# A last projection by seven products of half blocks, with sums of its weights prepared beside earlier stages

## The chip, the cores and the metric

The kernel runs on one core of one Trainium2 chip. The metric is the device time of one execution in microseconds; a kernel's time is the median of its runs. Only the last projection, the place where its weights are made ready, and the way one gated unit is written differ between the two kernels; inputs, outputs and all other stages are the same.

## What is computed

A layer of a streaming encoder: 2048 tokens of 1024 channels in float32, one layer, one batch. In the reference, cut to what matters:

```python
h = rms_norm(x, norm_g) * (1.0 + scale) + shift
u = h @ w_in
glu_in, gate_a, q, k, v, gate_b, m_a, m_b = split(u)
y_a = conv_branch(glu_in, gate_a)              # GLU, causal convolution of width 31, LayerNorm, projection
o   = stick_breaking_attention(norm(q), norm(k), v)
y_b = (o * silu(gate_b)) @ w_sb_out
y   = sigmoid(m_a) * y_a + sigmoid(m_b) * y_b
x   = x + gate * (y @ w_out)                   # w_out: 1024 x 1024
```

The last line is the last projection. Its product has the shape 1024 x 1024 by 1024 x 2048 in the kernel's orientation (channels on partitions, tokens along the free axis).

## The kernel before

Every large product is made of float32r halves: an operand is split into `hi`, its rounded value, and `lo`, what is left, and a product takes three matmuls (hi by hi, hi by lo, lo by hi; `mm3`). ScalarE casts `hi`, and GpSimd (for weights) or VectorE (for the rest) subtracts `lo`. Tokens go in four chunks of 512 (`CH`, `NCH`), channels in eight blocks of 128 (`KC`).

Weights come in **pieces** of 128 x 1024 (`piece`, `load_piece`, `split_into`): each half of 512 columns is loaded by SyncE into a `wl` tile (two of these, shared by all pieces), cast into `whi` (L102) and subtracted into `wlo` (L103). There are three slots for split pieces: two in the pool `wpa`, one in `wpb`, taken in turn, so a piece takes the slot that the third piece before it had. A piece is issued as soon as a slot and the `wl` tiles are free, as far as the scheduler's order on each engine lets it. SyncE, ScalarE, GpSimd and VectorE work their instructions off in order: one that waits holds all behind it.

The stages, in the order of TensorE's work:

- the first stage: normalised input, and the projections `glu`, `silu_block` (gate A, part of gate B), queries, keys and values; VectorE works off the convolution's taps beside it. `glu(j)` makes one channel block of the gated unit: `B_GLU_B` goes through a sigmoid on ScalarE (L660), `B_GLU_A` is multiplied with it on VectorE (L667). Both write `u`, whose even and odd tokens lie apart, as the convolution wants them
- the stage beside the LayerNorm, from about 620 to 780 us: `v_group(5)`, `gate_b(2)`, `gate_b(3)`, and three merge gates (`merge_gate`, of `blocks[:NEARLY]`). A generator `ln_all` puts a step of the LayerNorm after each of their tiles; it loads the convolution's output (`cv`), squares it (`sq`, L800), sums and casts (`hl`, L770), normalises, gates, and stores `za` (L834). Each gate tile is read by ScalarE into `vsg` (L857, L868) and stored (L859, L869)
- attention, with the other merge gates as a filler on TensorE in an order written out by hand; at its end the first chunk's `y_tiles`
- the tail. For each chunk: `y_tiles` (192 matmuls `p` by the weights `wc`, L1066 to L1072 for the evictions and the splitting of y into `yh` and `yl`), then eight output tiles, `out_tile` (24 matmuls `po` each, 192 for the chunk), evicted by one VectorE operation that multiplies by `gate` and adds x (L1083). The projection's weights `wo` are loaded and split once, in the first chunk (L1191), and stay: `wo0` in the pool `wr`, the others in `wor`, which is declared for the right side of the memory

In the tail TensorE alternates: y of chunk 0, output of chunk 0, y of chunk 1, and so on.

## Time and profile before

| | us |
|---|---|
| median of three runs | 1858.18 |
| lowest and highest run | 1856.52, 1859.29 |
| the profiled execution | 1858.59 |
| its span in the trace | 1856.5 |

The page gives each engine's busy time as a share of the span, then its chain of waits: from the last instruction back to what released it, step by step. A row of a group has the line, the engine, the operation, the tile written and those read, the count, the busy time and the mean of one, and the idle time of that engine ahead of it with what ended it. PE is TensorE's matmuls, PEld its weight loads, DVE VectorE, ACT ScalarE, POOL GpSimd, SP SyncE; a name such as SPq is that engine's queue. Rows of a timeline have start, duration, engine, line, operation, tiles, count and the idle time ahead. A matmul of 512 columns shows 0.39 us in such a row, but matmuls overlap: the step from one start to the next is what counts.

### The profile page before, as it was taken

How to read it: one execution, taken by the hardware profiler on the slowest of the kernel's cores; microseconds unless marked ns; L12 is line 12 of the kernel's file. 1: busy time of each engine (PE TensorE's matmuls, PEld its weight loads, DVE VectorE, ACT ScalarE, POOL GpSimd, SP SyncE). 2: the span in 40 equal slices, each digit the busy share in tenths (PEclk: the TensorE clock that was granted, in tenths of full speed). 3: DMA queues.
4: the chain of work that ended last, by engine and by line, in shares of the span. 5: the costliest groups of instructions: out<-in, count | busy, mean ns of one | idle time of the engine just before them, and what ended most of it. 6: DMA issues, size and time to landing. Idle time of an engine off the chain costs nothing.

```text
span 1856.5 us, 27230 instructions
## 1 busy us (share of the span) xinstructions
PE 1788.4 (96%) x9612; PEld 1510.5 (81%) x9612; DVE 1229.2 (66%) x1696; ACT 825.9 (44%) x1896; POOL 668.6 (36%) x883
## 2 busy tenths in 40 slices
PE   6899999999999999999999999999999899999999
PEld 5888889899898888788787777778788677888887
DVE  7645578888879555377777777767777895334241
ACT  5465113232131234377777776767777752010110
POOL 0253112112111133276656666666666731010100
PEclk9999999999999999999999999999999999999999
DMA  8563402315042454423231323231322446353532
GB/s 286 175 188 103 142 29 68 104 50 167 23 119 92 146 189 150 160 80 104 62 95 65 100 67 99 78 94 55 100 71 83 140 155 210 102 164 93 167 93 80
DMA packets 117596, 211.08 MB, mean 114 GB/s; under 512 B 15442, under 2 KB 27730, under 8 KB 117460
## 3 DMA queue, kind: packets, MB, share of 16 engines
q1 hardware_dynamic: 116308, 207.24, 35.9%
q10 hardware_dynamic: 1152, 2.10, 0.3%
q8 instruction: 76, 1.25, 0.3%
q14 instruction: 60, 0.49, 0.1%
HBM read 137.98 MB, written 71.30 MB: 113 GB/s over the span
## 4 chain that ended last, share of the span: by engine, by line
PE 77%; DVE 7%; POOL 5%; ACT 4%; issue 4%; DMA 3%; SPq 0%; DVEq 0%; ACTq 0%; POOLq 0%
PE pd L115 43%; PE po L115 9%; PE p L115 8%; PE av L115 5%; PE pT L120 5%; PE z L115 5%; POOL w L962 3%; DVE sc L955 3%; DMA wl<-in_w_qkv_dram 1%; DVE tlo L989 1%; ACT z L951 1%; POOL wlo L103 1%; PE pt L120 1%; ACT w L950 1%; DMA qst<-qhi 1%
## 5 line engine op out<-in xcount | busy, mean ns | idle before, releaser
L962 POOL TENSOR_TENSOR w<-w,sc 128x512 f32<-128x512 f32 (+1 forms) x320 | 361.4, 1130 | 252.6 <-DVE sc L955 179.5
L115 PE MATMUL pd<-hhi,whi 128*128 128x512 f32 x1024 | 410.6, 401 | 1.0 <-ACT vsg L868 1.0
L115 PE MATMUL pd<-hhi,wlo 128*128 128x512 f32 x1024 | 400.9, 391 | 0.0
L115 PE MATMUL pd<-hlo,whi 128*128 128x512 f32 x1024 | 400.6, 391 | 0.0
L955 DVE TENSOR_TENSOR_SCAN sc<-z,sc,w 128x512 f32<-128x512 f32 x192 | 244.9, 1279 | 91.3 <-ACT z L951 83.3
L103 POOL TENSOR_TENSOR wlo<-wl,whi 128x512 fp32r<-128x512 f32 x88 | 131.4, 1502 | 406.8 <-ACT whi L102 405.6
L950 ACT ACTIVATE w<-z 128x512 f32<-128x512 f32 (+1 forms) x320 | 172.3, 538 | 126.6 <-PE z L115 102.8
L115 PEld LDWEIGHTS pd<-hhi,wlo 128*128 128x128 f32 x1024 | 192.2, 188 | 41.6 <-POOL wlo L103 0.2
L115 PEld LDWEIGHTS pd<-hhi,whi 128*128 128x128 f32 x1024 | 194.0, 189 | 34.9 <-ACT vsg L868 1.4
L115 PEld LDWEIGHTS pd<-hlo,whi 128*128 128x128 f32 x1024 | 192.9, 188 | 33.9
L989 DVE TENSOR_TENSOR tlo<-pT,thi 128x512 fp32r<-128x512 f32 (+1 forms) x320 | 184.0, 598 | 35.4 <-ACT thi L988 32.9
L115 PE MATMUL z<-kt,q 128*128 128x512 f32 (+2 forms) x640 | 193.0, 383 | 5.5 <-DVE sc L955 4.0
L988 ACT CAST thi<-pT 128x512 fp32r<-128x512 f32 (+1 forms) x320 | 165.2, 527 | 61.2 <-PE pT L120 57.5
L120 PE MATMUL pT<-ident,w 128*128 128x128 f32 x1088 | 173.1, 275 | 9.7 <-POOL w L962 9.4
L120 PEld LDWEIGHTS pT<-ident,w 128*128 128x128 f32 x1088 | 137.4, 141 | 45.6 <-POOL w L962 14.5
L115 PE MATMUL pd<-whi,hhi 128*128 128x256 f32 x608 | 169.7, 287 | 3.7 <-ACT hhi L131 2.0
L951 ACT ACTIVATE z<-z 128x512 f32<-128x512 f32 (+1 forms) x320 | 171.8, 537 | 0.0
L115 PE MATMUL pd<-whi,hlo 128*128 128x256 f32 x608 | 167.0, 285 | 2.5 <-DVE hlo L131 1.9
L115 PE MATMUL pd<-wlo,hhi 128*128 128x256 f32 x608 | 154.0, 284 | 0.0
L959 DVE TENSOR_TENSOR_SCAN sc<-z,tri 128x512 f32<-128x512 f32 (+3 forms) x128 | 104.3, 819 | 60.9 <-ACT z L951 40.4
L115 PE MATMUL av<-tlo,vt 128*128 128x512 f32 (+1 forms) x320 | 122.8, 384 | 13.4 <-DVE tlo L989 10.2
L115 PEld LDWEIGHTS z<-kt,q 128*128 128x128 f32 x640 | 109.5, 189 | 25.4 <-DVE sc L955 6.4
(284 smaller groups left out, 3104.8 us busy)
## 6 DMA issues: line engine op xcount, KB each, us to landing
wl<-in_w_in_dram SPq DMA_DIRECT2D x64, 256.0 KB, 2.9
wa<-in_w_ada_dram SPq DMA_DIRECT2D x24, 512.0 KB, 5.2
wl<-in_w_qkv_dram SPq DMA_DIRECT2D x36, 256.0 KB, 2.8
xt<-in_x_n_dram SPq DMA_DIRECT2D x16, 512.0 KB, 5.5
vst<-st SPq DMA_DIRECT2D x64, 128.0 KB, 2.0
kt<-kst SPq DMA_DIRECT2D x32, 256.0 KB, 2.8
vt<-vst SPq DMA_DIRECT2D x32, 256.0 KB, 2.7
q<-qst SPq DMA_DIRECT2D x32, 256.0 KB, 2.8
```

What stands on the lines that cost most here:

```text
L103: (lo_eng or nc.gpsimd).tensor_tensor(out=lo[:, s], in0=wl, in1=f(hi[:, s]), op=ALU.subtract)
L115: i = nc.tensor.matmul(*a, **k)
L120: i = nc.tensor.transpose(*a)
L950: nc.scalar.activation(out=w[:, lo:], in_=z[:, lo:], func=AF.Sigmoid, scale=HD ** -0.5)
L951: nc.scalar.activation(out=z[:, lo:], in_=z[:, lo:], func=AF.Sigmoid, scale=-HD ** -0.5)
L955: nc.vector.tensor_tensor_scan(out=s[:, 1:], data0=z, data1=w, initial=s[:, 0:1], op0=ALU.mult, op1=ALU.bypass)
L959: nc.vector.tensor_tensor_scan(out=s[:, lo + 1:], data0=z[:, lo:], data1=tri[:, :CH - lo], initial=1.0, op0=ALU.mult, op1=ALU.max)
L962: nc.gpsimd.tensor_tensor(out=w[:, lo:], in0=w[:, lo:], in1=s[:, lo:CH], op=ALU.mult)
L988: nc.scalar.copy(out=thi[:, :n], in_=pT[:, :n])
L989: nc.vector.tensor_tensor(out=tlo[:, :n], in0=pT[:, :n], in1=f(thi[:, :n]), op=ALU.subtract)
```

## The change

**The last projection** works on pairs of chunks. The 1024 x 1024 weight matrix is cut into 2 x 2 blocks of 512, y of a pair of chunks into 2 x 2 blocks of 512 channels by 512 tokens. The table `SEVEN` gives for each of seven products the blocks of the weights that it sums (A), those of y (B), and the outputs to which it is added or from which it is subtracted. Blocks are named (row or input half, column half, sign); a product of one block each has a single term. A product is four row blocks of four input blocks, three matmuls each: 48. Each result is added by VectorE into one or two of the outputs (12 additions of four row blocks for a pair), with `gate` or its negative `ngate`; an output tile `acc` starts as x and is stored after its last product (`LASTS`). y stays in float32 and isn't split by itself.

**Operands.** A of five products is a sum of two blocks. These are made ahead: `prepare` loads two half tiles of `w_out` for each, adds them on GpSimd, splits the sum, and stores the pair to memory (`ws`, 512 KB); ten calls make two each. Four calls stand in the first stage (two in `glu(0)`, one in the first `silu_block`, one in `glu(1)`), six in the stage beside the LayerNorm (one behind each call of `v_group`, `gate_b` and `merge_gate`). Each takes one of the three slots for pieces, and `wl` tiles. A of the two other products (4 and 3) is loaded from `w_out` when it is used and split then. B is summed on GpSimd where it has two terms, cast on ScalarE and subtracted on VectorE. The operands of the next product are issued ahead of the current one; two sets of tiles (`za`, `zb` and `oa`, `ob`) take turns.

**The gated unit.** `glu` now reads PSUM by parity and writes `u` contiguously, where before it read PSUM in sequence and wrote `u` with a step.

```diff
+    SEVEN = {
+        2: (((1, 0, 1), (1, 1, 1)), ((0, 0, 1),), ((1, 0, 1), (1, 1, -1))),
+        1: (((0, 0, 1), (1, 1, 1)), ((0, 0, 1), (1, 1, 1)), ((0, 0, 1), (1, 1, 1))),
+        6: (((1, 0, 1), (0, 0, -1)), ((0, 0, 1), (0, 1, 1)), ((1, 1, 1),)),
+        4: (((1, 1, 1),), ((1, 0, 1), (0, 0, -1)), ((0, 0, 1), (1, 0, 1))),
+        7: (((0, 1, 1), (1, 1, -1)), ((1, 0, 1), (1, 1, 1)), ((0, 0, 1),)),
+        3: (((0, 0, 1),), ((0, 1, 1), (1, 1, -1)), ((0, 1, 1), (1, 1, 1))),
+        5: (((0, 0, 1), (0, 1, 1)), ((1, 1, 1),), ((0, 0, -1), (0, 1, 1))),
+    }
+    LASTS = {(1, 0): 4, (1, 1): 3, (0, 0): 5, (0, 1): 5}
+    H = KC // 2
...
+        sums = [(m, j) for m in SEVEN if len(SEVEN[m][0]) == 2 for j in range(H)]
+
+        def prepare():
+
+            npiece[0] += 1
+            pool = wpb if npiece[0] % 3 == 0 else wpa
+            for t in [pool.tile([P, 2, CH], F32R, tag=t, name=t) for t in ("whi", "wlo")]:
+                m, j = sums.pop(0)
+                w = [wpa.tile([P, CH], F32, tag="wl", name="wl", bufs=2) for _ in range(2)]
+                for i, (r, c_, _) in enumerate(SEVEN[m][0]):
+                    nc.sync.dma_start(w[i], w_out[j + H * r][:, c_ * CH:(c_ + 1) * CH])
+                nc.gpsimd.tensor_tensor(
+                    out=w[0], in0=w[0], in1=w[1],
+                    op=ALU.add if SEVEN[m][0][1][2] > 0 else ALU.subtract)
+                nc.scalar.copy(out=t[:, 0, :], in_=w[0])
+                nc.gpsimd.tensor_tensor(out=t[:, 1, :], in0=w[0], in1=f(t[:, 0, :]),
+                                        op=ALU.subtract)
+                ws_d[m, j] = dram(f"ws{m}_{j}", [P, 2, CH], F32)
+                nc.sync.dma_start(ws_d[m, j], f(t))
...
                 def at_(g):
-                    return u[:, :, g * CH // 2:(g + 1) * CH // 2].rearrange("p t m -> p m t")
+                    return u[:, :, g * CH // 2:(g + 1) * CH // 2]
+
+                def by_parity(ps):
+                    return ps.rearrange("p (m t) -> p t m", t=2)
 
                 w = piece(w_in[B_GLU_B + j])
+                if j < 2:
+                    prepare()
...
-                    nc.scalar.activation(out=at_(g), in_=ps.rearrange("p (m t) -> p m t", t=2),
-                                         func=AF.Sigmoid)
+                    nc.scalar.activation(out=at_(g), in_=by_parity(ps), func=AF.Sigmoid)
...
                 w = piece(w_in[B_GLU_A + j])
+                if j < 1:
+                    prepare()
...
-                    nc.vector.tensor_tensor(out=at_(g), in0=ps.rearrange("p (m t) -> p m t", t=2),
-                                            in1=at_(g), op=ALU.mult)
+                    nc.vector.tensor_tensor(out=at_(g), in0=by_parity(ps), in1=at_(g),
+                                            op=ALU.mult)
...
             def silu_block(blk, dst, after=None):
                 w = piece(w_in[blk])
+                if blk == B_GA:
+                    prepare()
...
             def v_group(grp):
                 w2 = [piece(w_qkv[grp, i]) for i in range(2)]
+                prepare()
...
             def gate_b(j):
                 w = piece(w_in[B_GB + j])
+                prepare()
...
             def merge_gate(blk, dst):
                 w = piece(w_in[blk])
+                prepare()
...
-            return yp.tile([P, CH], F32, tag="io", name=name, bufs=4)
+            return yp.tile([P, CH], F32, tag="io", name=name, bufs=8)
...
-                nc.vector.tensor_tensor(out=ma, in0=ma, in1=mb, op=ALU.add)
-                hi = yp.tile([P, CH], F32R, tag=f"yh{j}", name=f"yh{j}")
-                lo = yp.tile([P, CH], F32R, tag=f"yl{j}", name=f"yl{j}")
-                nc.scalar.copy(out=hi, in_=ma)
-                nc.vector.tensor_tensor(out=lo, in0=ma, in1=f(hi), op=ALU.subtract)
-                y[0].append(hi)
-                y[1].append(lo)
+                y[ch, j] = (yr if ch % 2 else yp).tile([P, CH], F32, tag=f"y{j}", name=f"y{j}")
+                nc.vector.tensor_tensor(out=y[ch, j], in0=ma, in1=mb, op=ALU.add)
                 yield
 
-        def out_tile(ch, j, y, psum):
...
+        def operands(m, ch):
+
+            q = "zo"[turn[0] % 2]
+            turn[0] += 1
+            A, B = [], []
+            for j in range(H):
+                A.append(operand(q, "a", j))
+                if (m, j) in ws_d:
+                    nc.sync.dma_start(f(A[j]), ws_d[m, j])
+                else:
+                    (r, c_, _), = SEVEN[m][0]
+                    w = io("w")
+                    nc.sync.dma_start(w, w_out[j + H * r][:, c_ * CH:(c_ + 1) * CH])
+                    split_z(w, A[j], (nc.gpsimd, nc.vector)[j % 2])
+            for kc in range(H):
+                B.append(operand(q, "b", kc))
+                t = combined(SEVEN[m][1], lambda t: y[ch + t[1], kc + H * t[0]],
+                             lambda: yp.tile([P, CH], F32, tag="io", name="sum", bufs=8),
+                             nc.gpsimd)
+                nc.scalar.copy(out=B[kc][:, 0, :], in_=t)
+                nc.vector.tensor_tensor(out=B[kc][:, 1, :], in0=t, in1=f(B[kc][:, 0, :]),
+                                        op=ALU.subtract)
+            return A, B
...
+        def product(m, ch, A, B, psum):
+            for j in range(H):
+                ps = psum("po")
+                for kc in range(H):
+                    s = slice(kc * P, (kc + 1) * P)
+                    mm3(ps, A[j][:, 0, s], A[j][:, 1, s], B[kc][:, 0, :], B[kc][:, 1, :],
+                        kc == 0, kc == H - 1)
+                for r, c_, sign in SEVEN[m][2]:
+                    row, g = j + H * r, ch + c_
+                    ts_ = slice(g * CH, (g + 1) * CH)
+                    if (row, g) not in acc:
+                        acc[row, g] = ya.tile([P, CH], F32, tag="acc", name="acc", bufs=12)
+                        nc.sync.dma_start(acc[row, g], x_t[row][:, ts_])
+                    o = acc[row, g]
+                    nc.vector.scalar_tensor_tensor(
+                        out=o, in0=ps, scalar=(gate if sign > 0 else ngate)[:, row:row + 1],
+                        in1=o, op0=ALU.mult, op1=ALU.add)
+                    if LASTS[r, c_] == m:
+                        nc.sync.dma_start(out_t[row][:, ts_], o)
...
-            for j in range(KC):
-                if ch == 0:
-                    wo[j] = resident(wr if j == 0 else wor, w_out[j], f"wo{j}")
-                out_tile(ch, j, y, psum)
+        for ch in (0, 2):
             if ch:
-                y = ([], [])
-                ygen = y_tiles(ch, za, zb, psum, y)
...
+                za3, zb3 = load_za(3), load_zb(3)
+                steps(y_tiles(2, za, zb, psum, y))
+                steps(y_tiles(3, za3, zb3, psum, y))
+            order = list(SEVEN)
+            nxt = operands(order[0], ch)
+            for i, m in enumerate(order):
+                A, B = nxt
+                if i + 1 < len(order):
+                    nxt = operands(order[i + 1], ch)
+                elif ch == 0:
+                    za, zb = load_za(2), load_zb(2)
+                product(m, ch, A, B, psum)
```

What stands where. First ScalarE's rows beside the LayerNorm, from the last tile of `v_group` through gate B 2 up to the start of gate B 3. Before (`st` is the value tile's cast, `vsg` a gate tile; `whi_6949` is gate B 3's piece, `whi_7174` the first merge gate's):

```order
L102 CAST whi_6949<-wl_6951 128x512
L102 CAST whi_6949<-wl_6955 128x512
L329 CAST st_6717<-pd_6668 128x8x64
L102 CAST whi_7174<-wl_7176 128x512
L857 ACTIVATE vsg_6789<-pd_6764 128x512
L102 CAST whi_7174<-wl_7180 128x512
```

and then, after eight rows of the LayerNorm:

```order
L857 ACTIVATE vsg_6851<-pd_6826 128x512
L800 ACTIVATE sq0_6867<-cv0_6523 128x512
L800 ACTIVATE sq1_6870<-cv1_6525 128x512
L800 ACTIVATE sq2_6873<-cv2_6527 128x512
L857 ACTIVATE vsg_6916<-pd_6891 128x512
L800 ACTIVATE sq3_6876<-cv3_6529 128x512
L770 CAST hl_6888<-t1_6883 128x512
L102 CAST whi_7359<-wl_7361 128x512
L857 ACTIVATE vsg_6945<-pd_6920 128x512
L102 CAST whi_7359<-wl_7365 128x512
```

In the change, the same stretch from the second tile of gate B 2 (L906 is the gate tile's sigmoid, L847 the square, L817 the cast `hl`, L233 the cast of a prepared sum; `whi_7069` is gate B 3's piece):

```order
L906 ACTIVATE vsg_6971<-pd_6946 128x512
L233 CAST wlo_6865<-wl_6875 128x512
L847 ACTIVATE sq0_6987<-cv0_6623 128x512
L847 ACTIVATE sq1_6990<-cv1_6625 128x512
L847 ACTIVATE sq2_6993<-cv2_6627 128x512
L906 ACTIVATE vsg_7036<-pd_7011 128x512
L847 ACTIVATE sq3_6996<-cv3_6629 128x512
L906 ACTIVATE vsg_7065<-pd_7040 128x512
L817 CAST hl_7008<-t1_7003 128x512
L102 CAST whi_7069<-wl_7071 128x512
L102 CAST whi_7069<-wl_7075 128x512
L233 CAST whi_7079<-wl_7081 128x512
```

Gate B 3's casts stood ahead of gate B 2's first tile; now they stand behind all of its four tiles and behind `hl`.

SyncE there in the change (`ws` is the store of a prepared sum, `wl_7071` and `wl_7075` are the loads of gate B 3's piece, `gb2_1` gate B 2's third tile, L787 the LayerNorm's next input):

```order
L881 DMA za2_3_274<-lsg_6933 128x512
L237 DMA ws6_3_6882<-wlo_6865 128x1024
L881 DMA za3_3_278<-lsg_6940 128x512
L908 DMA gb2_2_193<-vsg_6971 128x512
L787 DMA cv2_6982<-cv2_165 128x2x256
L787 DMA cv3_6984<-cv3_166 128x2x256
L908 DMA gb2_1_192<-vsg_7036 128x512
L101 DMA wl_7071<-in_w_in_dram 128x512
L101 DMA wl_7075<-in_w_in_dram 128x512
L829 DMA gt_7128<-ga0_2_169 128x512
L829 DMA gt_7128<-ga1_2_173 128x512
L829 DMA gt_7131<-ga2_2_177 128x512
```

Before, gate B 3's loads stand ahead of all stores of gate B 2; now they stand behind the third one.

The same place one stage on, the loads of the third merge gate in the change (`wl_7713`, `wl_7717`; `mb0_2` is the second tile of the gate before it):

```order
L829 DMA gt_7681<-ga1_0_171 128x512
L881 DMA za2_1_272<-lsg_7506 128x512
L881 DMA za3_1_276<-lsg_7513 128x512
L237 DMA ws5_1_7547<-wlo_7530 128x1024
L919 DMA mb0_3_234<-vsg_7574 128x512
L829 DMA gt_7684<-ga2_0_175 128x512
L919 DMA mb0_2_233<-vsg_7622 128x512
L829 DMA gt_7684<-ga3_0_179 128x512
L101 DMA wl_7713<-in_w_in_dram 128x512
L101 DMA wl_7717<-in_w_in_dram 128x512
```

They too stand behind stores of the gate that runs then, and of the LayerNorm's `za`.

TensorE where the tail begins, before (y of the first chunk, then the first output tile):

```order
L115 MATMUL p2_16451<-zb2_15675,wc7h_16350 128x512 x2
L115 MATMUL p2_16451<-zb2_15675,wc7l_16351 128x512
L115 MATMUL p2_16451<-zb3_15683,wc7h_16350 128x512 x2
L115 MATMUL p2_16451<-zb3_15683,wc7l_16351 128x512
L115 MATMUL po_16535<-yh0_15937,wo0h_16523 128x512
L115 MATMUL po_16535<-yl0_15938,wo0h_16523 128x512
```

and in the change, where the first product begins:

```order
L115 MATMUL p2_16956<-ob2_16573,wc7h_16589 128x512 x2
L115 MATMUL p2_16956<-ob2_16573,wc7l_16590 128x512
L115 MATMUL p2_16956<-ob3_16581,wc7h_16589 128x512 x2
L115 MATMUL p2_16956<-ob3_16581,wc7l_16590 128x512
L115 MATMUL po_17024<-zb0_16984,za0_16976 128x512 x3
L115 MATMUL po_17024<-zb1_16987,za0_16976 128x512 x3
L115 MATMUL po_17024<-zb2_16990,za0_16976 128x512 x3
L115 MATMUL po_17024<-zb3_16993,za0_16976 128x512 x3
```

Those last rows of `p` are now y of the second chunk: both chunks of a pair are done before their seven products, and a product's matmuls take as weights a half of `za` (a sum of `w_out`) and as moving tile a half of `zb` (a block of y).

More of the change, by code (lines that the diff above doesn't have):

```diff
@@ L162, in trunk_kernel @@
     za_d = [[dram(f"za{j}_{g}", [P, CH], F32) for g in range(NCH)] for j in range(JC)]
+    ws_d = {}
     o_d = [[dram(f"o{j}_{g}", [P, CH], F32) for g in range(NCH)] for j in range(JC)]
@@ L1004, in av_mm @@
                 nc.sync.dma_start(o_d[h // 2][rc][a], oc[a])
-        wcs, wo = {}, {}
+        wcs = {}
         def resident(pool, src, name):
@@ L1015, in io, with split_z, operand @@
         def io(name):
-            return yp.tile([P, CH], F32, tag="io", name=name, bufs=4)
-        def split_z(o, t):
+            return yp.tile([P, CH], F32, tag="io", name=name, bufs=8)
+        def split_z(o, t, eng=nc.vector):
             nc.scalar.copy(out=t[:, 0, :], in_=o)
-            nc.vector.tensor_tensor(out=t[:, 1, :], in0=o, in1=f(t[:, 0, :]), op=ALU.subtract)
+            eng.tensor_tensor(out=t[:, 1, :], in0=o, in1=f(t[:, 0, :]), op=ALU.subtract)
+        def operand(q, half, i):
+            pool = yr if (q, half) == ("o", "b") else yp
+            return pool.tile([P, 2, CH], F32R, tag=f"{q}{half}{i}", name=f"{q}{half}{i}")
         def load_za(ch):
@@ L1024, in load_za @@
             for kc in range(JC):
-                t = yp.tile([P, 2, CH], F32R, tag=f"za{kc}", name=f"za{kc}")
+                t = operand("zooz"[ch], "a", kc)
                 o = io("n")
@@ L1034, in load_zb @@
             for kc in range(JC):
-                t = yp.tile([P, 2, CH], F32R, tag=f"zb{kc}", name=f"zb{kc}")
+                t = operand("zooz"[ch], "b", kc)
                 o = io("o")
@@ L1075, in y_tiles @@
-                yield
-        def out_tile(ch, j, y, psum):
-            ts_ = slice(ch * CH, (ch + 1) * CH)
-            xt = io("xt")
-            nc.sync.dma_start(xt, x_t[j][:, ts_])
-            ps = psum("po")
-            dense(ps, wo[j], y, KC)
-            nc.vector.scalar_tensor_tensor(out=xt, in0=ps, scalar=gate[:, j:j + 1], in1=xt,
-                                           op0=ALU.mult, op1=ALU.add)
-            nc.sync.dma_start(out_t[j][:, ts_], xt)
+                y[ch, j] = (yr if ch % 2 else yp).tile([P, CH], F32, tag=f"y{j}", name=f"y{j}")
@@ new lines, in y_tiles, with combined @@
+                nc.vector.tensor_tensor(out=y[ch, j], in0=ma, in1=mb, op=ALU.add)
+                yield
+        def combined(terms, part, tmp, eng):
+            if len(terms) == 1:
+                return part(terms[0])
+            t = tmp()
+            (a, b) = terms
+            eng.tensor_tensor(out=t, in0=part(a), in1=part(b),
+                              op=ALU.add if b[2] > 0 else ALU.subtract)
+            return t
+        turn = [0]
+        def operands(m, ch):
[20 more added lines that the diff above has]
+            return A, B
@@ new lines, in trunk_kernel @@
+        acc = {}
+        def product(m, ch, A, B, psum):
[17 more added lines that the diff above has]
+                        nc.sync.dma_start(out_t[row][:, ts_], o)
@@ L1101, in trunk_kernel @@
         nf = ny = 0
-        prev = held = ygen = wr = yp = None
-        y = ([], [])
+        prev = held = ygen = wr = yp = ngate = None
+        y = {}
         psum = lambda n: pd.tile([P, CH], F32, tag="pd", name=n)
@@ L1125, in others @@
             def others(q, half):
-                nonlocal nf, ny, ygen, wr, yp
+                nonlocal nf, ny, ygen, wr, yp, ngate
                 while nf < (int(due[2 * q + half + 1] + 0.001) if q < LAST else NF):
@@ L1140, in others @@
                         wcs[1] = load_piece(wpa, w_cs[1])
+                    ngate = yp.tile([P, KC], F32, name="ngate")
+                    nc.vector.tensor_scalar(out=ngate, in0=gate, scalar1=-1.0, scalar2=None,
+                                            op0=ALU.mult)
                     ygen = y_tiles(0, za, zb, lambda n: psum(n), y)
@@ L1176, in trunk_kernel, with steps @@
     with s3:
-        wor = s3.enter_context(tc.tile_pool(name="wor", reuse_waits="tile", bufs=1, side="right"))
+        yr = s3.enter_context(tc.tile_pool(name="yr", reuse_waits="tile", bufs=1, side="right"))
         pd = s3.enter_context(tc.tile_pool(name="pd3", reuse_waits="tile", bufs=2, space=PSUM))
         psum = lambda n: pd.tile([P, CH], F32, tag=n, name=n, bufs=4 if n == "po" else 2)
-        for ch in range(NCH):
-            if ch:
-                y = ([], [])
-                ygen = y_tiles(ch, za, zb, psum, y)
-            for _ in ygen:
-                pass
-            if ch + 1 < NCH:
-                za = load_za(ch + 1)
-                zb = load_zb(ch + 1)
-            for j in range(KC):
-                if ch == 0:
-                    wo[j] = resident(wr if j == 0 else wor, w_out[j], f"wo{j}")
-                out_tile(ch, j, y, psum)
+        def steps(gen):
+            for _ in gen:
+                pass
+        za, zb = load_za(1), load_zb(1)
+        steps(ygen)
+        steps(y_tiles(1, za, zb, psum, y))
+        ya = s3.enter_context(tc.tile_pool(name="ya", reuse_waits="tile", bufs=1, side="right"))
+        for ch in (0, 2):
+            if ch:
+                za3, zb3 = load_za(3), load_zb(3)
[10 more added lines that the diff above has]
+                product(m, ch, A, B, psum)
 def _layout(i):
```

## The prediction

> **What bounds the kernel now.** I read the busy shares and the chain that ended last first, then busy time by stretch of the stages that the change touches, then the chain over the last 320 us, and last single rows of the engines where PE's weights are made ready.
>
> ```profile
> PE 1788.4 (96%) x9612; PEld 1510.5 (81%) x9612; DVE 1229.2 (66%) x1696; ACT 825.9 (44%) x1896; POOL 668.6 (36%) x883
> ...
> PE pd L115 43%; PE po L115 9%; PE p L115 8%; PE av L115 5%; PE pT L120 5%; PE z L115 5%; POOL w L962 3%; DVE sc L955 3%; DMA wl<-in_w_qkv_dram 1%; DVE tlo L989 1%; ACT z L951 1%; POOL wlo L103 1%; PE pt L120 1%; ACT w L950 1%; DMA qst<-qhi 1%
> ```
>
> PE is busy for 96% of the span; nothing else comes near. A matmul taken away is worth its step wherever PE doesn't wait, and a wait added in front of PE costs in full. By stretch (us, busy of PE, PEld, DVE, ACT, POOL, clock, DMA share, GB/s):
>
> ```profile
> 200.00:250.00 50.00, 50.00 (x222) 41.39 (x221) 35.48 (x36) 6.79 (x10) 7.06 (x4) 1.00 0.21 72
> 657.60:674.00 16.40, 16.40 (x78) 13.54 (x78) 12.78 (x26) 8.43 (x13) 9.48 (x7) 1.00 0.63 199
> 674.00:690.00 16.00, 16.00 (x76) 13.38 (x75) 10.26 (x23) 5.18 (x10) 5.14 (x5) 1.00 0.77 240
> 690.00:720.00 30.00, 30.00 (x137) 24.92 (x136) 15.64 (x26) 11.52 (x19) 11.19 (x8) 1.00 0.47 152
> 720.00:752.00 32.00, 32.00 (x154) 26.85 (x153) 14.95 (x31) 13.09 (x22) 7.32 (x6) 1.00 0.38 137
> ```
>
> In the GLU stage (first row) and beside the LayerNorm (the others) PE never rests: the new preparation finds idle ACT and POOL there, but no idle PE that could swallow a late weight. In the tail, the row where the first output projection starts, then the chain (start, us, what):
>
> ```profile
> 1541.33 0.39 PE L115 MATMUL po<-yh,wo0h 128*128 128x512 f32 x1
> ```
> ```profile
> 1548.18 39.93 PE po L115 x170
> 1588.12 43.54 PE p L115 x192
> 1631.66 44.64 PE po L115 x192
> ...
> 1764.47 43.52 PE p L115 x192
> 1807.99 44.66 PE po L115 x192
> 1852.65 0.03 issue
> 1852.68 0.75 DVE xt L1083
> ```
>
> From 1588 us on it is matmuls alone: `p` (y, 192 of them) and `po` (last projection, 192) in turn, then one eviction and the store.
>
> **The change part by part.** *The tail.* The four projections take 46.8 (1541.33 to 1588.12; some of it waits for loads of `w_out`), 44.64, 44.64 and 44.66 us: 180.7. Seven products of 4 x 4 x 3 matmuls for each pair of chunks make 336; two pairs make 672 where 768 stood. Their step isn't in the trace, but both ends are:
>
> ```profile
> L115 PE MATMUL po<-yh,wo7l 128*128 128x512 f32 x32 | 12.7, 396 | 0.0
> ...
> L115 PE MATMUL po<-yh,wo0l 128*128 128x512 f32 x32 | 12.5, 390 | 0.0
> ```
>
> `p` goes at 43.52/192 = 0.2267 us; `po` at 44.64/192 = 0.2325, and of its weights `wo0`, the only one in a left-side pool, is as fast as `p`, the seven of the right-side pool 6 ns slower. The products' weights (`za`, `oa`) all lie in the left-side pool, so I take 0.2267; the moving half `ob` lies on the right, so 0.2333 stays as the other end. That makes 2 x 336 x 0.2267 = 152.3 us (156.8 at the other end): **28.4 us less** (23.9). After the last matmul two evictions stand where one stood (a product feeds up to two outputs): +0.75. Tail: **-27.7** (-23.2).
>
> That holds if operands are ready. One product lasts 48 x 0.2267 = 10.9 us. Prices:
>
> ```profile
> L1083 DVE SCALAR_TENSOR_TENSOR xt<-po,gate,xt 128x512 f32<-128x512 f32 x32 | 23.8, 750 | 102.2 <-PE po L115 89.5 <-DMA xt<-in_x_t_dram 7.9 <-DMA mb<-mb 4.8
> L1072 DVE TENSOR_TENSOR yl<-ma,yh 128x512 fp32r<-128x512 f32 x25 | 17.3, 692 | 18.2 <-ACT yh L1071 18.2
> ...
> L1040 POOL TENSOR_TENSOR o<-o,gb 128x512 f32<-128x512 f32 x12 | 16.8, 1406 | 200.3 <-DMA gb<-gb 90.3 <-DMA o<-o 75.9 <-ACT wo6h L102 34.0
> L1071 ACT CAST yh<-ma 128x512 fp32r<-128x512 f32 x25 | 15.5, 620 | 196.4 <-DVE ma L1068 196.4
> ...
> L1020 DVE TENSOR_TENSOR zb<-o,zb 128x512 fp32r<-128x512 f32 x12 | 9.7, 807 | 20.5 <-ACT zb L1019 20.2
> ```
>
> For a pair of chunks: DVE 48 evictions x 0.75 + 32 subtractions x 0.69 = 58.1 us of 76.2; POOL 20 sums and 4 subtractions x 1.41 = 34; ACT 36 casts x 0.62 = 22. Two operand sets alternate, so row j of A is reloaded when product i-1 is done with it and wanted a row less than two products later (19 us); a 512 KB load takes 5.2 us in the row below. B is wanted whole: a set is free when product i-1 ends, the sums can be made before, four casts and subtractions take 4 x 0.69 + 0.62 = 3.4 of 10.9 us.
>
> ```profile
> wa<-in_w_ada_dram SPq DMA_DIRECT2D x24, 512.0 KB, 5.2
> ```
> ```profile
> 25.00:40.00 15.00, 12.95 (x100) 12.43 (x100) 13.04 (x24) 9.97 (x20) 0.00 (x0) 1.00 0.96 336
> ```
>
> Loads and stores of the first pair (8.4 MB of prepared sums, 2.1 of plain halves, x, output, next z) are about 19 MB in 76 us, 250 GB/s, where 336 went through at 0.96 share. So I cost operands at 0; the 32 casts and 32 subtractions of `yh` and `yl` that go save nothing, since PE covered them.
>
> *GLU by parity.* Its two operations now read PSUM at a step of 2 and write in sequence:
>
> ```profile
> L660 ACT ACTIVATE u<-pd x16: 1085/1108/1118, 172.5 to 474.2; 128x512 f32<-128x512 f32 x16
> ```
> ```profile
> L667 DVE TENSOR_TENSOR u<-pd,u x16: 1083/1098/1116, 197.9 to 495.7; 128x512 f32<-128x512 f32 x16
> ```
>
> At best each falls to a plain 0.60/0.68 (0.42 us less), at worst stays or doubles; PE at 50.00 of 50 hides either. 0; without that cover 32 x 0.42 = 13 us either way.
>
> *The preparation.* Ten calls make 20 half pieces of sums: 40 loads, 20 stores of 512 KB, 40 POOL operations, 20 casts. Their own time hides (POOL 4 x 1.29 = 5.2 us per call in stretches with 10 to 20 idle). What doesn't hide is room: each call takes one of three slots for split weights and both `wl` tiles, so the next piece, which was split two pieces ahead, now waits for a slot until one ahead, on SP and ACT behind work that has waits of its own. Four calls stand in the GLU stage, where SP and ACT are nearly idle: I reckon the next piece ready 2 to 5 us before PE asks, 0, bounded by 3 us each. Six stand beside the LayerNorm. Gate B 3, row by row, before:
>
> ```profile
> 657.58 0.48 PE L115 MATMUL pd<-hhi,whi 128*128 128x512 f32 x1
> ```
> ```profile
> 655.58 1.14 ACT L102 CAST whi<-wl 128x512 fp32r<-128x512 f32 x2 [3.74 <-PE pd L115]
> ...
> 679.66 0.63 ACT L800 ACTIVATE sq<-cv 128x512 f32<-128x512 f32 x1 [3.94 <-DMA za<-lsg]
> 680.20 0.58 ACT L857 ACTIVATE vsg<-pd 128x512 f32<-128x512 f32 x1
> ...
> 684.45 0.62 ACT L770 CAST hl<-t 128x512 fp32r<-128x512 f32 x1 [3.16 <-DVE t L749]
> ```
> ```profile
> 681.53 0.33 SPq L859 DMA_DIRECT2D gb<-vsg  x1
> ```
> ```profile
> wl<-in_w_in_dram SPq DMA_DIRECT2D x6, 256.0 KB, 3.2
> ```
>
> Gate B 2 starts at 657.58 and has 96 matmuls at 0.2267 and about 1.1 us of LayerNorm ones, so gate B 3 starts near 680.5; its casts were done at 655.58 (gate B 2's take that place in the change: cast by 656.2, subtracted on POOL by 657.5, in time for its third matmul). In the change gate B 3's two loads stand on SP behind the store at 681.53, which waits for `vsg` at 680.20, and that for the LayerNorm's `sq`, held 3.94 us by a store. Loads issue at 681.9 and 682.2 and land 3.2 later, the first at 685.1; the casts stand behind `hl` (to 685.1), so 685.7, and the first POOL half is done 1.29 later, 687.0. PE's third matmul needs it, at 681.0: 6 us late, and the DMA share of 0.77 there with a 512 KB store and four new loads more makes that **8** (6 to 9). Of the three merge gates behind it, by the same count, the first is in time and the second has no slack, **1** (0 to 2). The third, before:
>
> ```profile
> 742.74 1.29 ACT L800 ACTIVATE sq<-cv 128x512 f32<-128x512 f32 x2 [2.22 <-DMA za<-lsg]
> ```
> ```profile
> 744.54 7.85 SPq L869 DMA_DIRECT2D mb<-vsg  x3
> ```
> ```profile
> 751.77 0.48 PE L115 MATMUL pd<-hhi,whi 128*128 128x512 f32 x1
> ```
>
> It starts at 751.77 and in the change its loads stand behind the first of those stores, whose `vsg` waits for that `sq`, and that for a `za` store; a sum and a subtraction of 1.29 each come before that store on POOL. So the loads issue 2.6 later than 744.9, land 3.2 later at 750.7, 1.91 for cast and subtraction makes 752.6, against a third matmul at 752.3; with DMA as busy as above I take **3.5** (0 to 7). All: **+12.5**, 6 to 18.
>
> **Sum.** 1858.59 (the profiled execution: span 1856.5 and 2.1 around it) - 27.7 + 12.5 = 1843.4; the median of the runs shown, 1858.18, is 0.4 below the profiled one: **1843 us**.
>
> **The rivals.** *All hidden* (1831): the loads are issued earlier than I read the queue, or DMA is quick enough. For it: 27.7 with nothing given back; against it: the 3.94 and 3.16 us waits above, which the new order puts ahead of the casts. *Every preparation holds its piece* (1852): six pieces lose 3.5 each, 1830.5 + 21, and the slower step and the GLU stage make up to 1857. For it: every piece has the same two `wl` tiles ahead of it; against it: a piece lasts 96 x 0.2267 = 21.8 us, and only where `vsg` waits for the LayerNorm do the loads come in its last quarter. *The products become DVE's* (slower): DVE's subtractions read two SBUF tiles while POOL makes the sums, as here:
>
> ```profile
> L830 DVE TENSOR_TENSOR lsg<-gt,cv x16: 697/1790/1811, 669.3 to 768.1; 128x512 f32<-128x512 f32 x16
> ```
>
> At 1.79 instead of 0.70 beside POOL, the 32 subtractions take 57.3, DVE 93.3 us of a pair against PE's 76.2: +17 twice, 1843 + 34 = 1877. It decides from a mean of 1.26 us (36 + 32 x 1.26 = 76.2) and makes the kernel slower from 1.55. Against it: beside L1040's POOL work the same subtraction took 0.807, and POOL is busy for 34 of 76 us. [...]
>
> **How the numbers follow.** Forecast 0.60, all hidden 0.15, every piece held 0.17 (0.07 of it beyond 1854.5), products DVE's 0.08 (0.02 of it only as far as no change). About 0.2%, 3.7 us, is what a measurement of this kernel can tell from no change: faster 0.85, same 0.09, slower 0.06. The range goes from everything hidden, 1831, to the tail at the slower step with 18 us of late weights: 1830.5 + 4.4 + 18 = 1853, and 1 of the GLU stage's bound, 1854.
>
> **What would show it.** Right: `po` comes to 672 matmuls at 0.227, PE without gaps from the second y on, and between 680 and 760 us one gap of 6 to 9 us before gate B 3, with a cast `whi` as its releaser, and a smaller one before the third merge gate; the attention stage unchanged but later. Wrong: gaps of PE before a product's first row, on a subtraction of `ob` or `zb` (then DVE or POOL is late) or on a load of `ws`; gaps in the GLU stage; a `po` step of 0.233; or no gap near 680.

## The result, and the profile after

| | us |
|---|---|
| before, median of 5 | 1858.18 (1856.52 to 1860.17) |
| after, median of 5 | 1876.31 (1870.66 to 1882.84) |
| ratio, 95% interval | 1.0092 (1.0063 to 1.0122) |
| profiled execution after, its span | 1882.84, 1881.1 |

The change makes the kernel slower, where 1843 us was forecast. The profiled execution is the slowest of the five, so the account below adds up to 24.6 us (1881.1 - 1856.5) and not to the 18 of the medians. The page after, engines and chain:

```profile
PE 1780.3 (95%) x9516; PEld 1503.2 (80%) x9516; DVE 1302.7 (69%) x1777; ACT 844.7 (45%) x1940; POOL 799.8 (43%) x971
...
PE 63%; DMA 9%; POOL 8%; DVE 8%; issue 5%; ACT 5%; SPq 1%; DVEq 0%; POOLq 0%; ACTq 0%
PE pd L115 32%; PE p L115 8%; PE po L115 7%; PE av L115 5%; PE pT L120 5%; PE z L115 5%; DMA wl<-in_w_out_dram 3%; POOL w L1012 3%; DVE sc L1005 2%; DMA wl<-in_w_in_dram 2%; POOL wlo L103 2%; POOL wl L230 1%; DMA wl<-in_w_qkv_dram 1%; ACT z L1001 1%; DMA gb<-gb 1%
```

PE has 96 matmuls fewer and is busy 8 us less, yet the span grew: the chain is PE for 63% of it where it was 77%, and loads of `w_out` and POOL's sums (L230) stand on it now. Busy time by stretch, in the columns of before:

```profile
600.00:650.00 50.00, 47.44 (x290) 43.03 (x289) 25.90 (x29) 10.10 (x17) 12.89 (x10) 0.97 0.51 173
650.00:700.00 50.00, 42.18 (x235) 36.38 (x234) 25.51 (x43) 16.56 (x27) 20.35 (x15) 0.93 0.60 201
700.00:750.00 50.00, 46.31 (x213) 37.91 (x211) 25.77 (x55) 17.17 (x29) 23.11 (x17) 0.96 0.58 195
750.00:800.00 50.00, 44.27 (x190) 35.82 (x190) 15.89 (x30) 19.07 (x31) 23.37 (x19) 0.91 0.54 179
```

From 650 to 750 us PE never rested before; now it does in each row, and the granted clock, 1.00 in all rows of before that the prediction showed, is 0.91 to 0.97. To see where time goes, I compare when the same instruction starts in both traces:

| instruction | before | after | later by | of which here |
|---|---|---|---|---|
| last product of the gated unit (L667, now L712) | 495.66 | 498.95 | 3.3 | 3.3 |
| first sigmoid of the filler (L911, now L961) | 781.52 | 818.08 | 36.6 | **33.3** |
| last sigmoid of the filler | 1457.79 | 1493.51 | 35.7 | -0.8 |
| first eviction of y of chunk 1 (L1066, now L1121) | 1590.90 | 1586.47 | -4.4 | -40.1 |
| first eviction of y of chunk 3 | 1767.23 | 1759.02 | -8.2 | -3.8 |
| end of the span | 1856.5 | 1881.1 | 24.6 | 32.8 |

The last three are a reordered tail. Without any wait they would be -46.8 (no first output between the first two y), -13.1 (43.54 + 76.17 + 43.52 for 176.33) and +32.3 (76.17 for 44.66, and one eviction). So the tail lost 6.6 us at the first y, 9.3 between y of chunks 1 and 3, 0.5 at the end.

The 33 us first. PE's rows where gate B 3 begins (start, duration, idle ahead with its end):

```profile
694.32 0.80 PE L115 MATMUL pd<-hhi,whi 128*128 128x512 f32 x1 [7.69 <-ACT whi L102]
694.91 0.63 PE L115 MATMUL pd<-hlo,whi 128*128 128x512 f32 x1
...
697.55 0.53 PE L115 MATMUL pd<-hhi,whi 128*128 128x512 f32 x1
697.92 0.40 PE L115 MATMUL pd<-hlo,whi 128*128 128x512 f32 x1
```

This is the gap that was forecast, 7.7 us for 8, but it costs more than its length: from 694.32 to 697.92 there are seven matmuls in 3.60 us, which at 0.2267 take 1.59. **After the gap PE starts slowly and loses 2.0 us more.** The granted clock (the column before the DMA share) shows why: it is about half for 3.7 us, then full:

```profile
694.30:698.00 3.70, 3.55 (x8) 2.40 (x9) 0.17 (x1) 0.49 (x1) 2.51 (x2) 0.52 0.46 159
698.00:702.00 4.00, 4.00 (x21) 3.29 (x19) 0.00 (x0) 0.00 (x0) 0.00 (x0) 1.00 0.40 129
```

The same follows at three more places of this stage, each line the first row behind a gap:

```profile
745.31 1.81 PE L115 MATMUL psb<-dg,ones 128*128 128x128 f32 x8 [1.94 <-DVE dg L802]
748.87 0.79 PE L115 MATMUL pd<-hhi,whi 128*128 128x512 f32 x1 [1.75 <-ACT whi L102]
...
779.85 0.80 PE L115 MATMUL pd<-hhi,whi 128*128 128x512 f32 x1 [4.12 <-ACT whi L102]
810.92 0.79 PE L115 MATMUL pd<-hhi,whi 128*128 128x512 f32 x1 [6.27 <-ACT vsg L918]
```

A fifth slow start stands at the end of the first stage, behind a gap of 2.56 us:

```profile
625.77 0.38 PE L115 MATMUL pd<-whi,hhi 128*128 128x256 f32 x1 [2.56 <-DVE sg L726]
```
```profile
625.70:630.00 4.30, 4.22 (x22) 4.23 (x23) 0.15 (x2) 0.00 (x0) 0.48 (x1) 0.60 0.92 317
```

PE's matmuls stand in the same order in both traces up to the filler, so the delay can be followed from one to the next. Of the 33.3 us, 23.9 come in the gaps (less what the same gaps took before) and 9.3 in the slow starts behind them: 1.4 at 625.77, 2.1 at 694.32, 2.5 at 745.31 and 748.87 together, 1.9 at 774.67 and 779.85, 1.4 at 810.92.

Why weights are late, by the kernel's chain of waits through that first gap and on to the next piece (start, us, what):

```profile
687.46 0.33 SPq L908
...
687.83 4.94 DMA wl<-in_w_in_dram
...
694.35 2.52 POOL wlo L103 x2
...
696.88 5.22 DMA wl<-in_w_out_dram
...
702.27 1.29 POOL wl L230
...
705.98 3.63 DMA wl<-in_w_out_dram
...
709.75 1.30 POOL wl L230
...
713.94 4.53 DMA wl<-in_w_in_dram
```

Gate B 2's store (SP, L908) goes out, then gate B 3's load; the next piece's load comes only at 713.94, behind two rounds of a preparation, each load, sum, cast, subtraction. All of them use the same two `wl` tiles in turn. In the tail the chain has this (the second line is the load of `gb` that PE waits for at 1720.00):

```profile
1628.44 57.34 PE po L115 x252
...
1711.00 4.96 DMA gb<-gb
...
1720.00 79.79 PE p L115 x336
1799.79 76.40 PE po L115 x336
```

A pair's 336 product matmuls take 76.40 us; where y of chunk 2 begins, its inputs (`gb`) are late: PE waits for 3.96 us, and the twelve matmuls behind that gap take 5.27 us (1720.00 to 1725.27) where 2.72 would do. The last of these loads goes out at 1710.95, behind an output store on SP, and DMA is at 0.92 share in that stretch, where the same pair began at 0.36:

```profile
1640.00:1660.00 20.00, 20.00 (x90) 16.52 (x89) 18.12 (x22) 5.64 (x11) 14.04 (x10) 1.00 0.36 114
...
1700.00:1720.00 20.00, 16.04 (x71) 12.67 (x69) 12.13 (x18) 5.29 (x9) 5.48 (x5) 0.96 0.92 314
```

### The profile page after: what moved, and what is told of

The parts are those of the page before. It is cut to its first block, busy times and chain, and to the rows that moved or that the text cites. A ratio compares the mean times of both kernels' runs of the same rounds, so it can differ in the third digit from the quotient of the medians.

```text
span 1881.1 us, 27438 instructions
## 1 busy us (share of the span) xinstructions
PE 1780.3 (95%) x9516; PEld 1503.2 (80%) x9516; DVE 1302.7 (69%) x1777; ACT 844.7 (45%) x1940; POOL 799.8 (43%) x971
## 4 chain that ended last, share of the span: by engine, by line
PE 63%; DMA 9%; POOL 8%; DVE 8%; issue 5%; ACT 5%; SPq 1%; DVEq 0%; POOLq 0%; ACTq 0%
PE pd L115 32%; PE p L115 8%; PE po L115 7%; PE av L115 5%; PE pT L120 5%; PE z L115 5%; DMA wl<-in_w_out_dram 3%; POOL w L1012 3%; DVE sc L1005 2%; DMA wl<-in_w_in_dram 2%; POOL wlo L103 2%; POOL wl L230 1%; DMA wl<-in_w_qkv_dram 1%; ACT z L1001 1%; DMA gb<-gb 1%
## 5 line engine op out<-in xcount | busy, mean ns | idle before, releaser
L103 POOL TENSOR_TENSOR wlo<-wl,whi 128x512 fp32r<-128x512 f32 x88 | 136.9, 1565 | 321.2 <-ACT whi L102 321.0
L120 PEld LDWEIGHTS pT<-ident,w 128*128 128x128 f32 x1088 | 137.6, 141 | 45.3 <-POOL w L1012 14.1
```

The source lines that it names most:

```text
L103: (lo_eng or nc.gpsimd).tensor_tensor(out=lo[:, s], in0=wl, in1=f(hi[:, s]), op=ALU.subtract)
L120: i = nc.tensor.transpose(*a)
```

## The experiments

**One part at a time.** The tail without the six preparations beside the LayerNorm (the twelve sums that they make are left out, and other prepared sums are loaded in their place), and the ten preparations without the tail. The edit of the first:

```diff
         def prepare():
+            if len(ws_d) >= 8:
+                for _ in range(2):
+                    ws_d[sums.pop(0)] = list(ws_d.values())[len(ws_d) % 8]
+                return
```

> The changed kernel without the six preparations beside the LayerNorm: the twelve sums that they made are left out, and the tail loads eight other prepared pairs in their place (same bytes, same instructions in the tail). Theory A (the time is lost where weights come late beside the LayerNorm, 33 us there in the changed kernel's trace, the rest of its loss at the first y and at the change from products to y): that stage is back within 4 us of before, the tail as in the changed kernel, total 1849 us (1844 to 1854). Theory B (the loss belongs to the seven products and their operands, and the late stage only shifts it): 1865 us or more.

> The kernel before with the ten preparations added, at the places where the change has them, and nothing else: the sums are stored and not used. Theory A: +33 us beside the LayerNorm and +3 ahead of it, so 1893 us (1886 to 1900). Theory C (most of that stall is taken back in the attention stage, which has gaps of its own): 1870 us or less.

Measured: the tail alone 1842.26 us (ratio 0.9917, 0.9902 to 0.9932), the preparations alone 1891.16 (1.0177, 1.0162 to 1.0192). In the traces the filler's first sigmoid comes at 782.21 and 815.05, against 781.52: the preparations bring 33.5 us up to there, and only 0.8 us of it is taken back (the last one is at 1490.49, 32.7 late). The tail alone was 7 us faster than theory A had it, below its range; in its trace y of chunk 1 to chunk 3 took 167.89 us, 4.7 less than after the change. The loss is the preparation's; B and C fall. Next the gated unit by itself, of which the edit shows the sigmoid (the product on VectorE is changed in the same way):

```diff
-                    nc.scalar.activation(out=at_(g), in_=ps.rearrange("p (m t) -> p m t", t=2),
-                                         func=AF.Sigmoid)
+                    nc.scalar.activation(out=at_(g), in_=by_parity(ps), func=AF.Sigmoid)
```

> The kernel before with the gated unit written by parity, and nothing else. Theory A and the prediction: hidden behind TensorE, 1858 us within 0.2%, the sigmoid and the product of the gated unit at 0.6 to 1.1 us each. Rival: reading PSUM at a step of 2 makes them longer than the tiles of TensorE allow, so that TensorE waits for a PSUM buffer: 1862 us or more.

Measured: 1857.2 us (0.9993, 0.9984 to 1.0002), no difference. Its two operations by group (busy us, mean ns):

```profile
L669 DVE TENSOR_TENSOR u<-pd,u 128x512 f32<-128x512 f32 x16 | 11.1, 691 | 30.4 <-PE pd L115 30.4
L663 ACT ACTIVATE u<-pd 128x512 f32<-128x512 f32 x16 | 9.5, 595 | 40.1 <-PE pd L115 39.9
```

Both went to the time of a plain one (0.60 us of L857's sigmoid and 0.68 of L679's product before, where these two took 1.10 each), and PE covers it.

**Is it the place?** All ten calls in the first stage, where SP and ACT are nearly idle (edit: the six calls taken out, and the conditions `j < 2`, `j < 1`, `blk == B_GA` widened):

> The changed kernel with all ten preparations in the first stage: one behind each piece of the four gated units and behind the first two silu blocks, none beside the LayerNorm. Result as the reference. Theory A (the preparation costs where the next piece waits behind the LayerNorm's work on SP and ACT): that stage as before, the first stage at most 2 us longer for each call, total 1852 us (1847 to 1860). Theory D (a preparation costs about 5 us wherever it stands, through its transfers and the pair of wl tiles): first stage +30 us, total 1875 us.

Measured: 1862.86 us (1.0018, 1.0007 to 1.003), between the two theories and 3 us above A's range. The stage beside the LayerNorm is as before, but the first stage is 18.8 us longer (last product of the gated unit at 514.48). There the convolution's taps on DVE take longer, shown by one group of them, before and then here:

```profile
L620 DVE SCALAR_TENSOR_TENSOR cc<-v,wsum,cc 128x1024 f32<-128x1024 f32 x56 | 79.5, 1420 | 0.0
```
```profile
L659 DVE SCALAR_TENSOR_TENSOR cc<-v,wsum,cc 128x1024 f32<-128x1024 f32 x56 | 93.1, 1662 | 0.0
```

DVE, 39.1 of 50 us busy from 250 to 300 us before, is full there, and POOL, 6.1 before, has 28.0:

```profile
250.00:300.00 50.00, 44.97 (x232) 38.37 (x232) 50.00 (x34) 11.41 (x44) 27.97 (x15) 0.93 0.34 111
```

What PE waits for from 180 to 520 us, where the same view of the kernel before lists no wait (us in all, times, longest):

```profile
PE pt L120 <- DVE qn L337: 4.4, 1, 4.4
PE pd L115 <- POOL wlo L103: 4.2, 7, 1.5
PE pd L115 <- ACT whi L102: 2.7, 3, 1.6
```

So a preparation isn't free in that stage either: the longest wait is for DVE, whose taps stand ahead of `qn`, and 6.9 us are for split weights.

**What a gap costs.** Sums of zero on POOL hold four pieces of the kernel before:

```diff
+            def held(w, n):
+                for _ in range(n):
+                    nc.gpsimd.tensor_tensor(out=w[1][:, :CH], in0=f(w[1][:, :CH]),
+                                            in1=zero.to_broadcast([P, CH]), op=ALU.add)
```

> The kernel before with four pieces of weights held back by idle sums on POOL (33, 31, 20 and 17 additions of zero to the low half), in the first stage where TensorE has no other waits: gaps of TensorE of about 2, 2, 6 and 3 us. Result as the reference. Theory R (after a gap of about 2 us or more TensorE starts again at half its clock, for some 3.6 us, and loses 2 us more): each gap delays what follows by its length and 2.0 us, 4 x 2 = 8 us in all beside the gaps, time about 1879 us. Rival (the slow steps after a gap are those of weights that come late, not of the gap): the delay is the gap's length alone, about 1871 us.

Measured: 1906.21 us in a single execution; the sums took longer than I had reckoned, each gap was larger, and there are six of them. So neither theory's time fits, and the trace has to decide. The first two held pieces, in PE's rows:

```profile
268.11 0.79 PE L115 MATMUL pd<-hhi,wlo 128*128 128x512 f32 x1 [14.45 <-POOL wlo L653]
...
387.05 0.79 PE L115 MATMUL pd<-hhi,wlo 128*128 128x512 f32 x1 [9.27 <-POOL wlo L653]
```

The gated unit's products after the first gap are 13.9 us late where they were 2.8 early: 16.7 for a gap of 14.45, so 2.2 more. Over all six gaps (45.3 us, less the 1.75 that the kernel before has at one of these places) the filler is 56.9 us later than the rows ahead of them: 13.3 more than the gaps, 2.2 for each on average. Singly they are 1.6 to 2.9 us, with 2.0 behind the longest gap, 2.9 behind one of 6.51 and 1.6 behind one of 3.08, so they don't follow the gap's length. The granted clock from 268 to 272 us is 0.50. Theory R holds for these gaps, of about 3 us and more; its 2 us as the shortest was not tried here.

**What holds the next piece.** The preparation sums in the slot that it takes, and leaves the two `wl` tiles to the pieces:

```diff
-                w = [wpa.tile([P, CH], F32, tag="wl", name="wl", bufs=2) for _ in range(2)]
+                w = [f(t[:, i, :]) for i in range(2)]
...
-                    out=w[0], in0=w[0], in1=w[1],
+                    out=w[1], in0=w[0], in1=w[1],
...
-                nc.scalar.copy(out=t[:, 0, :], in_=w[0])
+                nc.scalar.copy(out=t[:, 0, :], in_=w[1])
```

> The changed kernel, with each preparation done inside the slot tile that it takes: its two half tiles of weights are loaded into the slot, summed and split there, so that the pair of wl tiles is left to the pieces; places, sums and stores as in the change. Result as the reference. Theory W (the next piece is late because it stands behind a preparation in the turn of the two wl tiles, which is two round trips of load, sum, cast and subtraction): the loss beside the LayerNorm falls from 33 us to 10 or less, total 1853 us (1847 to 1860). Theory S (the slots and the order on SP and ACT, behind stores that wait for the LayerNorm, hold it): 25 us or more stay, total 1868 us or more.

Measured: 1856.18 us (0.9986, 0.9977 to 0.9996), 20 less than the change; the filler's first sigmoid is at 790.67, 9.2 late. Theory W holds: with the tiles free, gate B 3's two loads (658.50 and the first at 663.36) stand on SP ahead of gate B 2's first store (L908) again:

```profile
658.50 0.40 SPq L101 DMA_DIRECT2D wl<-in_w_in_dram  x1
...
663.36 1.15 SPq L101 DMA_DIRECT2D wl<-in_w_in_dram  x2
...
666.40 0.43 SPq L908 DMA_DIRECT2D gb<-vsg  x1
```

Most of what is left of the stage's loss is one wait of the LayerNorm's own sums, 5.2 us, with its slow start, 3.3:

```profile
756.81 1.76 PE pst L115 x8
```

It starts 5.0 us after the matmul ahead of it. The chain to it has a store of `za` (3.37 us) and DVE's work around it, and before that loads and sums of the preparation on POOL; which of these makes it late was not tested.

**Towards a faster one.** In place and spread over the first stage; the same with two loads moved in the tail; and the moved loads on e5:

```diff
                         za = load_za(0)
-                        zb = load_zb(0)
                         wcs[1] = load_piece(wpa, w_cs[1])
+                        zb = load_zb(0)
...
-                za3, zb3 = load_za(3), load_zb(3)
-                steps(y_tiles(2, za, zb, psum, y))
+                y2 = y_tiles(2, za, zb, psum, y)
+                for _ in range(2 * KC):
+                    next(y2)
+                za3, zb3 = load_za(3), load_zb(3)
+                steps(y2)
```

> The changed kernel with the preparation in place as in e5 and all ten calls in the first stage, each behind a piece that a single piece follows: gated units' B pieces (4), the first A piece, and five silu blocks. Result as the reference. Theory W with A: first stage at most 4 us longer, the stage beside the LayerNorm as before, the first y and the change from products to y as in the changed kernel: 1846 us (1841 to 1853). Theory D (a preparation costs by its transfers and sums wherever it is): 1855 us or more.

> As e7a, and two loads moved: the second piece of the first y's weights ahead of the inputs zb, and the inputs of chunk 3 behind half of y of chunk 2. Result as the reference. Theory L (the first y and the change from products to y lose 6 to 8 us each because those loads stand ahead of what TensorE waits for): 1837 us (1832 to 1843). Rival (other operands are as late, or the memory's rate there is what limits): as e7a within 2 us.

> e5 (the change with the preparation in place) and the two moved loads of e7b. Result as the reference. By the theory that each loss is its own: e5's time less the 5 us that the moved loads gave between e7a and e7b, 1851 us (1847 to 1855). Rival (that difference was the first stage's, which also moved between those two): 1856 us as e5.

Measured: 1874.57 (1.0085, 1.007 to 1.01), 1868.49 (1.0047, 1.0032 to 1.0062) and 1853.49 us (0.9965, 0.995 to 0.9979). The spread was a miss by 29 us, and its rival D, that a preparation costs wherever it is, fits the time: the filler begins 30.0 us late. PE waits 8.7 us for DVE's `qn`, and the largest gap stands at the end of the first stage,

```profile
650.33 0.58 PE L115 MATMUL pd<-whi,hhi 128*128 128x256 f32 x1 [14.30 <-DVE sg L725]
```

where silu blocks have one `sg` tile: its product comes late behind DVE's taps, and the next block waits for its store as well. With the moved loads the totals are 6 us (e7b) and 3 us (e9, inside its range) lower, but in e7b's trace the filler begins 5.1 us earlier than in e7a's, before any moved load can act. From chunk 1's y to chunk 3's, where the second one should show, it is 170.61 in e7a and 166.58 in e7b, but 171.50 in e5 and 170.35 in e9. How much each of the two gives stays open.

Then fewer calls: eight, eight and six sums are made at use in the tail, from two half tiles, and the rest prepared in place:

```diff
+                    ws = [half(a) for a in SEVEN[m][0]]
+                    if len(ws) == 2:
+                        nc.gpsimd.tensor_tensor(
+                            out=ws[0], in0=ws[0], in1=ws[1],
+                            op=ALU.add if SEVEN[m][0][1][2] > 0 else ALU.subtract)
+                    split_z(ws[0], A[j], (nc.gpsimd, nc.vector)[j % 2])
```

> Twelve sums prepared (products 1, 6 and 7) in place, by the four calls of the change in the first stage and the calls of v_group and gate B 2; the eight sums of products 2 and 5 are made at use in the tail from two half tiles each (a POOL sum, cast, subtraction on POOL and DVE in turn); the two moved loads of e7b. Result as the reference. By the theory so far (wl tiles free, few calls beside the LayerNorm, tail ready in time): LayerNorm stage +3, first y and the change from products to y +8, tail -28: 1841 us (1835 to 1848), faster than the kernel before. Rival (POOL with up to 12 us of sums in a product of 10.9, or DVE, becomes the tail's pace): 1850 us or more.

> As e8, with the twelve prepared sums those of products 2, 1 and 6, which are the first three of each pair, and those of products 7 and 5 made at use (7 with its subtractions on DVE). Result as the reference. In e8's trace the first product of each pair waits for its operands (2.5 us of gap and a slow start, at 1600 and 1770 us). Theory: both go, 1847 us (1843 to 1851). Rival (the products 7 and 5 then wait as long, since POOL's or DVE's work is the same): 1852 us or more.

> As e10, with one call more (gate B 3): fourteen sums prepared (products 2, 1, 6 and two rows of 7), six made at use (two rows of 7, and 5, subtracted on POOL and DVE in turn). Result as the reference. In e9 the calls of the merge gates cost 7 us of the 12.5 beside the LayerNorm and the earlier ones 5; in e10 POOL and DVE set the tail's pace in products 7 and 5. Theory: beside the LayerNorm +5, tail 4 us shorter than e10's: 1848 us (1844 to 1852). Rival (what is taken from the tail comes back beside the LayerNorm): 1853 us or more.

Measured: 1852.78 (0.9964, 0.9951 to 0.9977), 1851.93 (0.9963, 0.9949 to 0.9976) and **1845.03 us (0.9933, 0.9919 to 0.9946)**. The first fits its rival, the second lies between its theory (up to 1851) and its rival (from 1852). In both, the time from chunk 1's y to the end is 300.1 us where e9 has 292.5: eight sums at use make the tail wait. The last, with six, has 295.5 there, was forecast at 1848 and beats both kernels. Its calls, four in the first stage and those of `v_group`, gate B 2 and gate B 3, cost 2 us, where 5 were expected: from the last product of the gated unit to the filler's first sigmoid it is 287.8 us (before 285.9).

## Why the prediction was wrong, point by point

- **Products at 0.2267**: right. 76.40 / 336 = 0.2274 us; 672 matmuls, and those that read `ob`, on the right side, show the same mean in the profile as those that read `zb` (390 ns).
- **Operands at nothing**: wrong, 16 us (6.6 + 9.3 + 0.5). What was late is y, not a product. At the change from products to y, loads for the next chunk come together with prepared sums, x and output: I compared a mean of 250 GB/s with 336, but the pair starts at 114 and ends at 314 with 0.92 share. At the first y PE waits 5.03 us before 1514.35, in a chain over POOL's and DVE's work, and no run isolates the cause of that one.
- **DVE's pace, the slower rival**: not what happened; that its 1877 us lie so near the measured 1876 is chance. DVE's subtractions beside POOL's sums went from 0.69 to 1.05 us, under the 1.26 from which it decides:

```profile
L1159 DVE TENSOR_TENSOR ob<-sum,ob 128x512 fp32r<-128x512 f32 x20 | 20.7, 1051 | 1.9 <-ACT ob L1158 1.9
```

- **GLU by parity**: right, and hidden (e3).
- **Preparation in the first stage, 0**: nearly, 3.3 us after the change, 1.5 in e2. What I gave as the reason, SP and ACT idle, isn't the limit there when more calls come: DVE and late split weights are (e4).
- **Preparation beside the LayerNorm, +12.5**: the step that failed most; 33.3 us, and 33.5 in e2 less 1.5 of the first stage. With the operands it makes up the miss: in the spans 39.8 us, of which 20.8 here, 16.6 in the tail, 3.3 in the first stage, and 0.8 taken back. Its mechanism was right as far as it went: loads behind a gate's store that waits for the LayerNorm, 7.7 us for 8 before gate B 3, 4.1 for 3.5 before the third merge gate, 1.75 for 1 before the second. What was mis-sized: the LayerNorm's own matmuls (1.94 and 1.34) and the filler's first piece (6.27, before 0.98) were put at 0, as was the longer gap at 625.77, which makes the gaps 23.9, not 12.5; and **every gap's slow start was left out**, 1.4 to 2.5 us each at five places, the other 9.3. The price could have been read in the trace of before: at the end of attention, behind a gap of 1.26 us and several smaller ones, the granted clock is 0.52. The gap of 1.75 us at the end of the first stage has no slow start behind it, as the steps are 0.12 us from the second matmul on:

```profile
1463.50:1467.00 3.50, 3.46 (x12) 2.70 (x13) 2.81 (x4) 2.24 (x6) 3.44 (x4) 0.52 0.67 226
```
```profile
621.67 0.39 PE L115 MATMUL pd<-whi,hhi 128*128 128x256 f32 x1 [1.75 <-DVE sg L679]
621.89 0.28 PE L115 MATMUL pd<-whi,hlo 128*128 128x256 f32 x1
622.01 0.27 PE L115 MATMUL pd<-whi,hhi 128*128 128x256 f32 x1
```

- **Why the loads came late**: half right. I named the slot; e5 shows that the pair of `wl` tiles, with two round trips of a preparation ahead of each piece, is what put the loads behind those stores.
- **All hidden** (1831): not even the tail alone came to it (1842 in e1). **Every piece held** (1852) has the right stage and too small a price. Of the signs, the `po` step, the gap before gate B 3, the smaller one before the third merge gate and the unchanged attention came as forecast; PE without gaps from the second y on did not, by the gap at 1720.00.

## What to carry to other kernels

Work that is put beside a stage takes that stage's buffers in turn: count the round trips through the smallest pool that the next weights share, not the engines' idle time. Where TensorE is the bound, the waits of 2.56 to 14.45 us that were followed in these traces cost their length and about 2 us for the start after it (1.4 to 3.3), so several of them weigh more than their sum. Shorter waits are less sure: one of 1.75 us cost its length alone, one of 1.26 among smaller ones was followed by a slow start. And sums on GpSimd weren't free beside VectorE's taps, however idle GpSimd looked: from 250 to 300 us it went from 6.1 to 28.0 us busy in e4, and one group of taps from 1420 to 1662 ns each.
